# The last projection's column pair: other PSUM banks, and its first column's square sums and scalings behind the tail's splits

## The chip, the cores and the metric

The kernel runs on one core of a Trainium2 chip. The metric is the time of one execution on the device in microseconds (us). Before the change the median of three runs is 1376.21 us (1376.1 to 1376.72). A core has TensorE (PE, matrix products), VectorE (DVE), ScalarE (ACT), GpSimd (POOL) and SyncE (SP); the last two only issue transfers in the part of the program that matters here. Matrix products end in PSUM, 8 banks of 128 x 512 floats; VectorE and ScalarE read them from there.

## The reference

A trunk of two layers on 256 tokens of width 2048: one of gated linear attention, one of retention, each ahead of its own output projection and residual add, and one RMS norm at the end. The change touches only the last steps, in the second layer:

```python
    return (o * jax.nn.silu(gate)) @ w_out
...
            h = h + retention_mixer(rms_norm(h, ret_norm[j]), positions, ret_w_in[j],
                                    ret_gn_g[j], ret_gn_b[j], ret_w_out[j])
    return rms_norm(h, final_norm)
```

The final norm divides each token's row by the root of its mean square over all 2048 columns and multiplies by `final_norm`.

## The kernel before

**Precision.** A float32 product is done as three products of rounded parts. ScalarE rounds a weight block to its upper part (`hi`, L298), VectorE subtracts to get the lower part (`lo`, L299); this is "the split" of a weight block (128 x 1024, two k-tiles of 512 columns), written by `emit_split`. TensorE then multiplies x_hi by hi, x_hi by lo and x_lo by hi (L340 to L342 in `mm3`, L411 to L413 in `three`). So each step of TensorE needs `hi` for its first matmul and `lo` for its second. The `hi` and `lo` pools have four buffers each; splits are written up to three steps ahead (`LOOK`). Raw weight blocks come by transfers on SP's queue, each waiting for a buffer that a split has read; where two column blocks are combined, GpSimd's queue adds one block to another in a transfer (L310) or VectorE does (L293).

**The output projection.** Its 4096 rows are done in two halves of 2048; the last one (`out_last`, `out_tail`) makes four column blocks of 512 for two halves of tokens (t = 0, 1), and a step `j` covers 256 rows:
- column 0, steps 0 to 5; then column 3, steps 0 to 3 (`part`, 4 = `HEAD`); then column 0's last two steps. Column 3's part is added to the residual rows `rb_resid` at L1073, column 0's sums by `out_cols` (add L960, square sum L599, scaling by `final_norm` L964).
- columns 1 and 2 as a pair in `out_pair`, called with c = 1, g = 2. For the first half of its rows (steps 0 to 3) it makes seven products of sums and differences instead of eight (`product`, 12 matmuls each); the other steps 4 to 7 go directly (`direct`, 12 matmuls each). Four accumulators, B, A, C and V1, each take one PSUM bank: C and V1 gather column c, B and A gather column g, and A also serves for single products that are read at once. `join` adds a bank into `rb_resid` (L990) or subtracts (L992); `u3` is a copy of A by ScalarE (L1029).
- `whole(col, t)` finishes a block of a column: the square sum over it by ScalarE (L599, tile `sqj`, into `ssum`) and its scaling by `final_norm` on VectorE (L999).
- the tail: column 3's steps 4 to 7. Its four splits are written inside the pair, before direct step 7, in an extra loop: upper parts in `xhl`, lower ones in tiles `tail`. `out_tail` runs t = 0 in one bank (24 matmuls of 512) and t = 1 in two half-wide ones (48 of 256), and after each evacuates (L1142), squares (L1144), forms the norm factor from `ssum` by way of `pre` (L1121, L1122), scales the four columns (L1160, L1162) and sends them out.

**Banks.** The pool `acc` has four banks under the tags acc0 to acc3, one buffer each: a new tile under a tag waits until the old one has been read. `slots` says which tag comes next. When `out_pair` is reached, column 0's two halves (t = 0, 1) are in acc2 and acc3, and column 3's part, already added by L1073, in acc0 and acc1.

```python
        slots.rotate(1)
        B, A, C, V1 = acc(4, f"{name}e{c}_ps", which=list(slots))
...
    slots = deque((1, 2, 3, 0))
```

The first two lines stand ahead of the pair, the last one ahead of the tail. So B, A, C, V1 are acc1, acc2, acc3, acc0, and the tail uses acc1 for t = 0, acc2 and acc3 for t = 1.

**Order.** A scheduler puts the instructions of each engine in order by its own estimate of their times; `keep` pins an instruction to the order in which it is written. Joins, the tail's splits and the pair's matmuls are pinned; square sums and scalings are not.

Of the kernel before, what the change touches and what calls it, by code (L numbers as in the profile page):

```python
# [15 lines left out]
ALU = mybir.AluOpType  # L16
# [162 lines left out]
def kernel(  # L179
# [18 lines left out]
    nc = tc.nc  # L198
# [20 lines left out]
    keep = tc.keep_in_program_order  # L219
# [9 lines left out]
    slots = deque(range(4))  # L229
# [13 lines left out]
    def block(key):  # L243
        return w_all[places[key]].rearrange("p (k n) -> p k n", n=GW)
# [21 lines left out]
    def emit_raws(c):  # L266
        c = cur["load"] = max(c, cur.get("load", 0))
        while emitted["raw"] < len(loads):
            n = emitted["raw"]
            h = held.get(bufs[n])  # L270
            if n > c and (n > c + DMA_LOOK + len(_spare(loads[n])) or (h is not None and last_use[h] >= emitted["sub"])):
                break
            emit_raw()

    def split_tiles(i):
        if i < last0:
            hi = hi_p.tile([P, SUB, GW], F32R, tag="hi", name=f"hi{i}")
            lo = lo_p.tile([P, SUB, GW], F32R, tag="lo", name=f"lo{i}")
            return hi, lo
        j = i - last0  # L280
        hi = xhl[:, j * SUB : (j + 1) * SUB].rearrange("p k a t -> p k (a t)")
        return hi, t4_p.tile([P, SUB, GW], F32R, tag="t4", name=f"tail{j}")

    def emit_split(pieces=1, between=None):
        i = emitted["sub"]
        c, pre, post = subs[i]
        emit_raws(c)
        src = raws[c]
        for n in range(i + 1, min(i + 1 + EARLY, len(subs))):
            at, by = subs[n][:2]  # L290
            if by is not None and n not in added:
                added.add(n)
                nc.vector.tensor_tensor(raws[at], raws[at], raws[by], ALU.add)  # L293
        hi, lo = split_tiles(i)
        step = SUB // pieces
        for k in range(pieces):
            sl = slice(k * step, (k + 1) * step)
            a = nc.scalar.activation(hi[:, sl], src[:, sl], AF.Copy)  # L298
            b = nc.vector.tensor_tensor(lo[:, sl], src[:, sl], hi[:, sl].bitcast(F32), ALU.subtract)  # L299
            if i >= last0 - 4:  # L300
                keep(a)
                keep(b)
            if i == 0:
                first(a, b)
                if k == 0:
                    between()
        splits[i] = (hi, lo)
        emitted["sub"] += 1
        for n, key in post:
            nc.gpsimd.dma_start(raws[n], block(key), accum_op=ALU.add)  # L310
        emit_raws(c)
# [13 lines left out]
    def drain_side():  # L325
        while side:
            advance()

    def next_weights():
        i = state["sub"]  # L330
        while emitted["sub"] <= min(i + LOOK, len(subs) - 1):
            emit_split()
        state["sub"] += 1
        return splits.pop(i)
# [72 lines left out]
    def three(ps, xh, xl, hi, lo, q, stop):  # L407
        start, again = id(ps) not in begun, {"skip_group_check": id(ps) in closed}
        begun.add(id(ps))
        pin = keep if cur.get("pin") else lambda x: x  # L410
        pin(mm(ps, xh, hi[:, q, :], start=start, stop=False, **again))  # L411
        pin(mm(ps, xh, lo[:, q, :], start=False, stop=False, **again))  # L412
        pin(mm(ps, xl, hi[:, q, :], start=False, stop=stop, **again))  # L413
        if stop:
            closed.add(id(ps))
# [8 lines left out]
    def direct(lhs, ps, j, stop=False):  # L424
        hi, lo = next_weights()
        for t in range(2):
            cols = slice(t * P, (t + 1) * P)
            for q in range(SUB):
                kt = j * SUB + q
                three(ps[t], lhs[:, kt, 0, cols], lhs[:, kt, 1, cols], hi, lo, q, stop and q == SUB - 1)  # L430
# [47 lines left out]
    def get_resid(name):  # L478
        r = rs_p.tile([P, 2, D], F32, tag="rs", name=name)
        nc.gpsimd.dma_start(r, cur["resid_at"])  # L480
        cur["resid"] = r
# [56 lines left out]
    def first(*ins):  # L538
        for x in ins:
            tc.stamp_issue_order_token(x.ins, "first")  # L540
# [55 lines left out]

    def square_sum(t, c):
        junk = sg_p.tile([P, GW], F32, tag="sg", name="sqj")
        nc.scalar.activation(  # L599
            junk, cur["resid"][:, t, c * GW : (c + 1) * GW], AF.Square, accum_out=ssum[:, t, c : c + 1]  # L600
        )

# [363 lines left out]
    fns = {}  # L966
# [10 lines left out]
    def out_pair(c, first, name, final=False):  # L977
        lhs, s = ogt, cur["s"]
        B, A, C, V1 = acc(4, f"{name}e{c}_ps", which=list(slots))
        slots.rotate(-2)  # L980
        onward = not (first or final)
        P5 = lev_p.tile([P, GW], F32, tag="lev", name=f"{name}e{c}_p5")
        plain = lambda kt0, t: lambda k, a: lhs[:, kt0 + k, a, t * P : (t + 1) * P]
        summed = lambda i: lambda k, a: s[i][:, k, a, :]
        u3 = t4_p.tile([P, 2, GW], F32, tag="t4", name=f"{name}e{c}_u3")[:, 0, :]

        def join(col, t, src, op=ALU.add):
            dst = cur["resid"][:, t, col * GW : (col + 1) * GW]
            if op == ALU.add:
                keep(nc.vector.tensor_tensor(dst, src, dst, ALU.add))  # L990
            else:
                keep(nc.vector.tensor_tensor(dst, dst, src, ALU.subtract))  # L992

        def whole(col, t):
            if not first:
                square_sum(t, col)
            if final:
                dst = cur["resid"][:, t, col * GW : (col + 1) * GW]
                nc.vector.tensor_tensor(dst, dst, fns[col], ALU.mult)  # L999

        late = deque([out_transposes(c)] if onward else [])

        def turn():
            advance()
            if late:
                next(late[0], None)

        g = c + 1
        cur["pin"] = final
        product(A, plain(0, 0), stop=True)  # L1010
        advance()
        direct(lhs, (C, V1), 4)
        join(g, 0, A)
        advance()
        product(C, summed(0))
        advance()
        direct(lhs, (C, V1), 5)
        drain_side()
        product(P5, summed(1), stop=True)
        direct(lhs, (C, V1), 6)  # L1020
        for t in range(2):
            join(c, t, P5)
        product(A, summed(2), stop=True)
        product(B, plain(4, 0))
        join(c, 0, A, ALU.subtract)
        direct(lhs, (C, V1), 7, stop=True)
        product(A, summed(3), stop=True)
        with tc.high_priority():
            keep(nc.scalar.activation(u3, A, AF.Copy))  # L1029
        join(c, 0, C)  # L1030
        whole(c, 0)
        direct(lhs, (B, A), 4)
        join(c, 1, u3, ALU.subtract)
        join(c, 1, V1)
        whole(c, 1)
        direct(lhs, (B, A), 5)
        turn()
        product(A, plain(4, 1))
        turn()
        direct(lhs, (B, A), 6)  # L1040
        turn()
        while final and emitted["sub"] < len(subs):
            emit_split()
        direct(lhs, (B, A), 7, stop=True)
        join(g, 0, B)
        whole(g, 0)
        join(g, 1, A)
        whole(g, 1)
        if onward:
            for _ in late[0]:  # L1050
                pass
            tasks.append(out_transposes(g))
        begun.clear()
        closed.clear()
# [5 lines left out]
    def out_last(name):  # L1060
        ps = acc(2, f"{name}0_ps")
        steps_x(ps, ogt, range(CUT), lambda j: step())
        part = acc(2, f"{name}3_ps")
        steps_x(part, ogt, range(HEAD), lambda j: step(), end=HEAD)
        get_resid(f"{name}_resid")
        for c in range(3):
            norm_row(c)
        steps_x(ps, ogt, range(CUT, NSUB), lambda j: step())
        while tasks:
            step()  # L1070
        for t in range(2):
            dst = cur["resid"][:, t, 3 * GW : 4 * GW]
            nc.vector.tensor_tensor(dst, part[t], dst, ALU.add)  # L1073
        for t in range(2):
            out_cols(0, ps[t], t, False, True)
        norm_row(3)
        slots.rotate(1)
        out_pair(1, False, name, True)

    def out_half(first, final, name, cut=0, hook=None, joint=(False, False)):  # L1080
# [357 lines left out]
    slots = deque((2, 3, 0, 1))  # L1438
    out_half(True, False, "ga", joint=JOINT["ao", 0])
    slots = deque((2, 3, 0, 1))  # L1440
# [4 lines left out]
    slots = deque((2, 3, 0, 1))  # L1445
# [8 lines left out]
    slots = deque((0, 1, 2, 3))  # L1454
# [7 lines left out]
    slots = deque((2, 3, 0, 1))  # L1462
    tasks.append(make_sums(ogt, "rsum2", sums_in_v))
    out_last("rb")
    slots = deque((1, 2, 3, 0))
# [104 lines left out]
```

## Time and profile before

| | us |
|---|---|
| median of three runs | 1376.21 |
| the profiled execution | 1375.77 |
| its span, first to last instruction | 1374.0 |
| TensorE busy in the span | 1362.7 (99%) |
| VectorE busy | 1100.2 (80%) |
| ScalarE busy | 846.5 (62%) |
| the last pair on TensorE, first to last start | 1311.69 to 1353.19 |
| the tail on TensorE, first to last start | 1354.44 to 1365.60 |

Times of the trace count from the span's start. A row of the timeline names start, length, engine, line and operation, output and inputs, with the idle time of the engine just ahead of it in brackets and what ended it. Matmuls overlap: one of 512 columns takes 0.39 us, but the next starts 0.23 us after it, so their rate is read from the starts.

### The profile page before, as it was taken

To read this page: it belongs to the slowest core of one execution; us is meant where nothing else is said; L and a number is where in the kernel's file an instruction comes from. 1 tells how busy PE (TensorE), PEld (TensorE's weight loads), DVE (VectorE), ACT (ScalarE), POOL (GpSimd) and SP (SyncE) were. 2 spreads that over 40 slices of the span, in tenths; PEclk is the share of its full clock that TensorE was granted. 3 is DMA by queue.
4 is the path that set the end of the run, shared out by engine and by line. 5 is a ranking of instruction groups with operands and counts; after the bars stand their busy time and mean duration, and the time that the engine had idled before them with its cause. 6 is when DMAs were issued, how large, how long until landed. Compare 5 with 4: busy or idle time off the path is not lost.

```text
span 1374.0 us, 18376 instructions
## 1 busy us (share of the span) xinstructions
PE 1362.7 (99%) x6564; PEld 1143.6 (83%) x6564; DVE 1100.2 (80%) x1523; ACT 846.5 (62%) x1115; POOL 136.8 (10%) x194
## 2 busy tenths in 40 slices
PE   9999999999999999999999999999999999999997
PEld 7888888888888888888888888888888888888886
DVE  6686795987878886769888888886858897889786
ACT  6576656656567747656666566655546666666554
POOL 1003020110021021001011010100101101010010
PEclk9999999999999999999999999999999999999999
DMA  9755566789658667868897878896798797879772
GB/s 369 250 171 168 173 202 184 162 246 323 191 155 271 198 206 191 303 168 241 277 312 200 257 204 248 208 327 205 185 361 236 214 273 191 262 194 332 221 181 107
DMA packets 84507, 315.03 MB, mean 229 GB/s; under 512 B 9776, under 2 KB 10800, under 8 KB 83136
## 3 DMA queue, kind: packets, MB, share of 16 engines
q1 hardware_dynamic: 67200, 241.63, 50.6%
q0 software_dynamic: 15920, 64.89, 24.0%
q10 hardware_dynamic: 1296, 7.35, 1.5%
q8 instruction: 51, 0.84, 0.2%
q14 instruction: 40, 0.33, 0.1%
HBM read 303.35 MB, written 10.49 MB: 228 GB/s over the span
## 4 chain that ended last, share of the span: by engine, by line
PE 96%; DMA 1%; DVE 1%; issue 1%; ACT 0%; POOL 0%; SPq 0%; DVEq 0%; POOLq 0%; ACTq 0%
PE rqk_ps L383 8%; PE re_ps L411 8%; PE re_ps L412 8%; PE re_ps L413 8%; PE rqk_ps L384 4%; PE gqk_ps L383 4%; PE gg_ps L341 3%; PE gv_ps L342 3%; PE gv_ps L340 3%; PE gv_ps L341 3%; PE gg_ps L340 3%; PE gg_ps L342 3%; PE ge_ps L412 2%; PE ge_ps L411 2%; PE ge_ps L413 2%; PE gae_ps L413 2%
## 5 line engine op out<-in xcount | busy, mean ns | idle before, releaser
L299 DVE TENSOR_TENSOR lo<-raw,hi 128x1024 fp32r<-128x1024 f32 (+1 forms) x567 | 687.2, 1222 | 213.7 <-ACT hi L298 202.9
L298 ACT ACTIVATE hi<-raw 128x1024 fp32r<-128x1024 f32 (+1 forms) x567 | 596.5, 1057 | 391.8 <-PE rqk_ps L383 48.7
L383 PE MATMUL rqk_ps<-xhl,hi 128*128 128x512 f32 x480 | 162.8, 397 | 0.0
L412 PE MATMUL re_ps<-lo,xhl 128*128 128x512 f32 x352 | 137.4, 390 | 0.0
L413 PE MATMUL re_ps<-hi,xhl 128*128 128x512 f32 x352 | 137.2, 390 | 0.0
L310 POOL DMA_DIRECT2D raw<-in_w_all x90 | 78.0, 868 | 556.3 <-DVE lo L299 291.0
L411 PE MATMUL re_ps<-hi,xhl 128*128 128x512 f32 x352 | 132.5, 391 | 0.0
L384 PE MATMUL rqk_ps<-xhl,lo 128*128 128x256 f32 x480 | 122.4, 280 | 0.0
L383 PEld LDWEIGHTS rqk_ps<-xhl,hi 128*128 128x128 f32 x480 | 89.6, 188 | 17.8
L384 PEld LDWEIGHTS rqk_ps<-xhl,lo 128*128 128x128 f32 x480 | 87.6, 189 | 3.4
L413 PEld LDWEIGHTS re_ps<-hi,xhl 128*128 128x128 f32 x352 | 66.1, 188 | 13.6
L412 PEld LDWEIGHTS re_ps<-lo,xhl 128*128 128x128 f32 x352 | 66.1, 188 | 13.2
L411 PEld LDWEIGHTS re_ps<-hi,xhl 128*128 128x128 f32 x352 | 66.0, 188 | 13.3
L383 PE MATMUL gqk_ps<-xhl,hi 128*128 128x512 f32 x216 | 76.6, 399 | 0.0
L341 PE MATMUL gg_ps<-lo,xhl 128*128 128x512 f32 x192 | 75.4, 393 | 0.0
L341 PE MATMUL gv_ps<-lo,xhl 128*128 128x512 f32 x192 | 75.2, 392 | 0.0
L340 PE MATMUL gv_ps<-hi,xhl 128*128 128x512 f32 x192 | 75.1, 393 | 0.0
L342 PE MATMUL gv_ps<-hi,xhl 128*128 128x512 f32 x192 | 75.1, 391 | 0.0
L342 PE MATMUL gg_ps<-hi,xhl 128*128 128x512 f32 x192 | 75.0, 391 | 0.0
L340 PE MATMUL gg_ps<-hi,xhl 128*128 128x512 f32 x192 | 74.8, 391 | 0.0
L828 POOL TENSOR_TENSOR s<-s,m 128x64 f32<-128x64 f32 x56 | 36.2, 676 | 232.6 <-DVE m L819 223.3
L384 PE MATMUL gqk_ps<-xhl,lo 128*128 128x256 f32 x216 | 59.1, 280 | 0.0
(434 smaller groups left out, 2656.6 us busy)
## 6 DMA issues: line engine op xcount, KB each, us to landing
raw<-in_w_all SPq DMA_DIRECT2D x449, 512.0 KB, 4.8
raw<-in_w_all POOLq DMA_DIRECT2D x90, 512.0 KB, 6.8
resid<-in_x_n SPq DMA_DIRECT2D x2, 1024.0 KB, 10.4
gg<-in_gn_g POOLq DMA_DIRECT2D x8, 256.0 KB, 4.2
resid_x<-resid ACTq DMA_DIRECT2D x1, 2048.0 KB, 8.0
gb<-in_gn_b POOLq DMA_DIRECT2D x8, 256.0 KB, 6.3
gb_resid<-resid_x POOLq DMA_DIRECT2D x1, 2048.0 KB, 11.4
resid_g<-gb_resid ACTq DMA_DIRECT2D x1, 2048.0 KB, 9.1
```

What stands on the lines that cost most here:

```text
L298: a = nc.scalar.activation(hi[:, sl], src[:, sl], AF.Copy)
L299: b = nc.vector.tensor_tensor(lo[:, sl], src[:, sl], hi[:, sl].bitcast(F32), ALU.subtract)
L310: nc.gpsimd.dma_start(raws[n], block(key), accum_op=ALU.add)
L340: pin(mm(ps, xh, hi[:, q, :], start=kt == begin, stop=False))
L341: pin(mm(ps, xh, lo[:, q, :], start=False, stop=False))
L342: pin(mm(ps, xl, hi[:, q, :], start=False, stop=kt == end - 1))
L383: mm(ps[c], wh, rhs[:, kt, :, :], start=kt == 0, stop=False)
L384: mm(ps[c][:, 0, :], wl, rhs[:, kt, 0, :], start=False, stop=False)
L411: pin(mm(ps, xh, hi[:, q, :], start=start, stop=False, **again))
L412: pin(mm(ps, xh, lo[:, q, :], start=False, stop=False, **again))
L413: pin(mm(ps, xl, hi[:, q, :], start=False, stop=stop, **again))
L828: nc.gpsimd.tensor_tensor(dst, dst, side_of(m[:, li, :], z), ALU.add)
```

## The change

`rotate(1)` becomes `rotate(-1)`: B, A, C, V1 are now acc3, acc0, acc1, acc2. The tail's banks stay what they were, so it now follows C (t = 0) and V1 and B (t = 1) in its banks. And in the last pair, `whole` of column c is held back: its two square sums and two scalings are written after the tail's splits, ahead of direct step 7, and are pinned, as are column g's.

```diff
     def square_sum(t, c):
         junk = sg_p.tile([P, GW], F32, tag="sg", name="sqj")
-        nc.scalar.activation(
+        return nc.scalar.activation(
             junk, cur["resid"][:, t, c * GW : (c + 1) * GW], AF.Square, accum_out=ssum[:, t, c : c + 1]
         )
...
-        def whole(col, t):
+        held_back = []
+
+        def whole(col, t, now=False):
+            if final and col == c and not now:
+                held_back.append((col, t))
+                return
             if not first:
-                square_sum(t, col)
+                a = square_sum(t, col)
             if final:
+                keep(a)
                 dst = cur["resid"][:, t, col * GW : (col + 1) * GW]
-                nc.vector.tensor_tensor(dst, dst, fns[col], ALU.mult)
+                keep(nc.vector.tensor_tensor(dst, dst, fns[col], ALU.mult))
...
         while final and emitted["sub"] < len(subs):
             emit_split()
+        for col, t in held_back:
+            whole(col, t, True)
         direct(lhs, (B, A), 7, stop=True)
...
-        slots.rotate(1)
+        slots.rotate(-1)
         out_pair(1, False, name, True)
```

On all engines the instructions are the same as before. SP's, GpSimd's and TensorE's stand in the same order; on ScalarE and VectorE only the two square sums and the two scalings move. Lines from 994 on have other numbers in the changed kernel (L999 is L1005, L1142 is L1150). The numbers behind a name count tiles and differ between the kernels too.

VectorE before, from C's join in the pair (`rbe_ps_11571`) to the join of B (`rbe_ps_11569`); `fn_11516` is column c's part of `final_norm`:

```order
L990 TENSOR_TENSOR rb_resid<-rbe_ps_11571,rb_resid 128x512
L999 TENSOR_TENSOR rb_resid<-rb_resid,fn_11516 128x512
L299 TENSOR_TENSOR lo_11789<-raw_11331,hi_11788 128x1024
L992 TENSOR_TENSOR rb_resid<-rb_resid,rbe_u_11574 128x512
L990 TENSOR_TENSOR rb_resid<-rbe_ps_11572,rb_resid 128x512
L999 TENSOR_TENSOR rb_resid<-rb_resid,fn_11516 128x512
L299 TENSOR_TENSOR lo_11810<-raw_11640,hi_11809 128x1024
L299 TENSOR_TENSOR lo_11826<-raw_11682,hi_11825 128x1024
L299 TENSOR_TENSOR tail_11835<-raw_11702,xhl 128x1024
L299 TENSOR_TENSOR tail_11844<-raw_11714,xhl 128x1024
L299 TENSOR_TENSOR tail_11859<-raw_11726,xhl 128x1024
L299 TENSOR_TENSOR tail_11862<-raw_11738,xhl 128x1024
```

`lo_11810` belongs to direct step 6 of B and A, `lo_11826` to step 7; B's join follows the last row. VectorE at the same place now:

```order
L990 TENSOR_TENSOR rb_resid<-rbe_ps_11571,rb_resid 128x512
L299 TENSOR_TENSOR lo_11786<-raw_11331,hi_11785 128x1024
L992 TENSOR_TENSOR rb_resid<-rb_resid,rbe_u_11574 128x512
L990 TENSOR_TENSOR rb_resid<-rbe_ps_11572,rb_resid 128x512
L299 TENSOR_TENSOR lo_11804<-raw_11640,hi_11803 128x1024
L299 TENSOR_TENSOR lo_11820<-raw_11682,hi_11819 128x1024
L299 TENSOR_TENSOR tail_11829<-raw_11702,xhl 128x1024
L299 TENSOR_TENSOR tail_11838<-raw_11714,xhl 128x1024
L299 TENSOR_TENSOR tail_11853<-raw_11726,xhl 128x1024
L299 TENSOR_TENSOR tail_11856<-raw_11738,xhl 128x1024
L1005 TENSOR_TENSOR rb_resid<-rb_resid,fn_11516 128x512 x2
L990 TENSOR_TENSOR rb_resid<-rbe_ps_11569,rb_resid 128x512
```

Both scalings have gone from between the joins and splits to behind the tail's four splits, and stand directly ahead of B's join. ScalarE's square sums move in the same way, from ahead of the upper splits `hi_11788` and `hi_11809` to behind the four that go to `xhl`, where all four of the pair now follow one another.

TensorE where the tail begins, with the engines whose semaphores a matmul waits for, before:

```order
L412 MATMUL rbe_ps_11570<-lo_11826,ogt 128x512
L413 MATMUL rbe_ps_11570<-hi_11825,ogt 128x512
L340 MATMUL tail_ps_11889<-xhl,ogt 128x512 [waits DVE_49,Activation_49]
L341 MATMUL tail_ps_11889<-tail_11835,ogt 128x512
L342 MATMUL tail_ps_11889<-xhl,ogt 128x512
```

and now:

```order
L412 MATMUL rbe_ps_11570<-lo_11820,ogt 128x512
L413 MATMUL rbe_ps_11570<-hi_11819,ogt 128x512
L340 MATMUL tail_ps_11889<-xhl,ogt 128x512 [waits Activation_49]
L341 MATMUL tail_ps_11889<-tail_11829,ogt 128x512 [waits DVE_49]
L342 MATMUL tail_ps_11889<-xhl,ogt 128x512
```

The tail's first matmul waited for VectorE's read of the bank as well as for its upper split; now it waits for the split alone, and the second one for its lower split. At the pair's start the wait for a bank moves likewise, from A's first matmul to V1's first, 18 matmuls later.

## Prediction

> **What bounds the kernel now.** I read the page first (its chain), then TensorE's waits over the last 74 us, where the change lies, then TensorE's rows around each wait, then VectorE's and ScalarE's rows in front of them. The chain says that TensorE sets the time:
>
> ```profile
> span 1374.0 us, 18376 instructions
> ...
> PE 96%; DMA 1%; DVE 1%; issue 1%; ACT 0%; POOL 0%; SPq 0%; DVEq 0%; POOLq 0%; ACTq 0%
> ```
>
> So only what makes TensorE stand still, or what follows its last matmul, is worth anything. TensorE's waits from 1300 us to the end are three (us in total, times, longest):
>
> ```profile
> PE tail_ps L340 <- DVE rb_resid L990: 0.9, 1, 0.9
> PE rbe_ps L412 <- DVE lo L299: 0.5, 1, 0.5
> PE rbe_ps L411 <- DVE rb_resid L960: 0.4, 1, 0.4
> ```
>
> All three lie inside the last pair or at its two edges. TensorE's rows around them (start us, us, what, idle before and what ended it):
>
> ```profile
> 1310.92 0.39 PE L342 MATMUL rb_ps<-hi,ogt 128*128 128x512 f32 x1
> 1311.69 0.47 PE L411 MATMUL rbe_ps<-hi,ogt 128*128 128x512 f32 x1 [0.38 <-DVE rb_resid L960]
> ...
> 1312.24 0.39 PE L413 MATMUL rbe_ps<-hi,ogt 128*128 128x512 f32 x1
> ...
> 1347.16 0.39 PE L411 MATMUL rbe_ps<-hi,ogt 128*128 128x512 f32 x1
> 1348.07 0.50 PE L412 MATMUL rbe_ps<-lo,ogt 128*128 128x512 f32 x1 [0.53 <-DVE lo L299]
> 1348.41 0.40 PE L413 MATMUL rbe_ps<-hi,ogt 128*128 128x512 f32 x1
> 1348.64 0.39 PE L411 MATMUL rbe_ps<-hi,ogt 128*128 128x512 f32 x1
> ...
> 1353.19 0.39 PE L413 MATMUL rbe_ps<-hi,ogt 128*128 128x512 f32 x1
> 1354.44 0.47 PE L340 MATMUL tail_ps<-xhl,ogt 128*128 128x512 f32 x1 [0.86 <-DVE rb_resid L990]
> ...
> 1354.98 0.39 PE L342 MATMUL tail_ps<-xhl,ogt 128*128 128x512 f32 x1
> ```
>
> The idle in brackets is less than a pause costs, since the first matmul behind it also starts its successor late. I therefore measure by starts. Undisturbed, starts are 0.227 us apart: between 1312.24 and 1347.16 lie 154 steps (13 steps of 12 matmuls, less two), and 34.92 / 154 = 0.2268. A pause is then the third start behind it, less the last start ahead, less 3 x 0.227 = 0.68:
> - pause 1, at the pair's start: 1312.24 - 1310.92 - 0.68 = 0.64
> - pause 2, at the lower split of direct step 6: 1348.64 - 1347.16 - 0.68 = 0.80
> - pause 3, at the tail's first matmul: 1354.98 - 1353.19 - 0.68 = 1.11
>
> Together 2.55 us. Between them TensorE has no more to give, as the table by stage shows (stretch, us, TensorE busy, weight loads, VectorE, ScalarE, GpSimd, granted clock, DMA share):
>
> ```profile
> 1312.00:1347.00 35.00, 35.00 (x156) 28.98 (x155) 29.80 (x32) 21.49 (x28) 4.03 (x5) 1.00 0.75 201
> 1354.40:1365.80 11.40, 11.36 (x72) 10.32 (x72) 6.53 (x21) 5.39 (x14) 0.00 (x0) 1.00 0.15 55
> ```
>
> **The change, part by part.** VectorE's rows that the three pauses hang on, and those behind:
>
> ```profile
> 1310.87 1.28 DVE L960 TENSOR_TENSOR rb_resid<-rb_ps,rb_resid 128x512 f32<-128x512 f32 x2
> ...
> 1340.07 0.68 DVE L990 TENSOR_TENSOR rb_resid<-rbe_ps,rb_resid 128x512 f32<-128x512 f32 x1
> 1341.55 0.69 DVE L999 TENSOR_TENSOR rb_resid<-rb_resid,fn 128x512 f32<-128x512 f32 x1 [0.79 <-ACT sqj L599]
> 1342.50 1.23 DVE L299 TENSOR_TENSOR lo<-raw,hi 128x1024 fp32r<-128x1024 f32 x1 [0.26 <-ACT hi L298]
> 1343.64 0.68 DVE L992 TENSOR_TENSOR rb_resid<-rb_resid,rbe_u 128x512 f32<-128x512 f32 x1
> 1344.36 0.69 DVE L990 TENSOR_TENSOR rb_resid<-rbe_ps,rb_resid 128x512 f32<-128x512 f32 x1
> 1345.84 0.69 DVE L999 TENSOR_TENSOR rb_resid<-rb_resid,fn 128x512 f32<-128x512 f32 x1 [0.79 <-ACT sqj L599]
> 1346.79 2.36 DVE L299 TENSOR_TENSOR lo<-raw,hi 128x1024 fp32r<-128x1024 f32 x2 [0.26 <-ACT hi L298]
> 1349.07 4.63 DVE L299 TENSOR_TENSOR tail<-raw,xhl 128x1024 fp32r<-128x1024 f32 x4
> 1353.61 0.69 DVE L990 TENSOR_TENSOR rb_resid<-rbe_ps,rb_resid 128x512 f32<-128x512 f32 x1
> ...
> 1358.08 0.15 DVE L1122 TENSOR_SCALAR pre<-pre 128x1 f32<-128x1 f32 x1
> 1360.17 0.76 DVE L1142 TENSOR_TENSOR rb_resid<-tail_ps,rb_resid 128x256 f32<-128x256 f32 x2 [1.94 <-PE tail_ps L342]
> ```
>
> *Banks at the pair's start (pause 1).* A's first product used to need the bank that L960 empties at 1310.87 to 1311.55; now it takes one that column 3's part left long before. The L960 bank goes to V1, whose first matmul is the 19th of the pair: 1311.15 + 18 x 0.227 = 1315.23, 3.7 us after it is free. Pause 1 goes whole: 0.64.
>
> *Supply between 1312 and 1347.* This gain lasts only if splits keep up with a TensorE that is 0.64 us ahead. ScalarE's and the transfers' rows:
>
> ```profile
> 1332.95 2.01 ACT L298 ACTIVATE hi<-raw 128x1024 fp32r<-128x1024 f32 x2 [0.85 <-DMA raw<-in_w_all]
> ...
> 1339.20 0.60 ACT L1029 ACTIVATE rbe_u<-rbe_ps 128x512 f32<-128x512 f32 x1 [0.30 <-PE rbe_ps L413]
> 1340.79 0.63 ACT L599 ACTIVATE sqj<-rb_resid 128x512 f32<-128x512 f32 x1 [0.99 <-DVE rb_resid L990]
> ...
> 1345.71 1.99 ACT L298 ACTIVATE hi<-raw 128x1024 fp32r<-128x1024 f32 x2
> 1347.61 3.89 ACT L298 ACTIVATE xhl<-raw 128x1024 fp32r<-128x1024 f32 x4
> ...
> 1357.27 1.28 ACT L1118 ACT_TABLE_LOAD   x1
> ```
>
> ```profile
> 1327.25 12.83 DMA raw<-in_w_all
> ```
>
> ```profile
> DMA packets 2, 0.02 MB, mean 1 GB/s; under 512 B 0, under 2 KB 0, under 8 KB 0
> ```
>
> The first row is the one split here that a transfer held up; its data go to the second half of the sixth product, which begins with the pair's 115th matmul, so TensorE wants the lower split at 1312.24 + 113 x 0.2268 = 1337.9. The split pair ends by about 1335.3 (hi at 1334.0, 1.2 more for the lower). With TensorE 0.64 ahead, 2.0 us remain: no cost. The last accumulated transfer (next fence) lands at 1327.25 + 12.83 = 1340.08. The last fence is all DMA from 1344.5 to 1363: two small packets, so every weight block of the tail has landed by 1344.5. No DMA is moved, and the queues of SP and GpSimd keep their order.
>
> *Square sums and scalings of the first column moved (pause 2).* Before, VectorE loses in front of direct step 6's lower split two scalings (0.6 each by starts) and two waits of 0.79 for the square sums; ScalarE loses 0.73 for each sum ahead of an upper split. In the changed order, with TensorE 0.64 earlier (times in the clock of these rows):
> - TensorE: direct 4 at 1339.00 - 0.64 = 1338.36, direct 6 at 1346.52 with its lower split wanted at 1346.75, the tail at 1346.52 + 24 x 0.227 = 1351.97.
> - ScalarE: the copy u3 ends 1339.16; the next upper split waits for the data, 1340.1 to 1341.15; that of direct 6 for the buffer which direct 4 frees, 1341.3 to 1342.35; that of direct 7 for direct 5, 1344.0 to 1345.05; four tail splits (3.89) to 1348.95; the two held-back sums to 1350.4.
> - VectorE: lower split 1341.2 to 1342.3, joins L992 and L990 to 1343.6, direct 6's lower split 1343.6 to 1344.8: 1.9 us before TensorE wants it. Pause 2 goes whole: 0.80. Direct 7's follows 1345.1 to 1346.25, the four tail splits to 1350.9, the two scalings to 1352.1.
>
> *Banks at the tail (pause 3).* The tail's first half used to need the bank of B, whose join at 1353.61 stood behind four tail splits. It now takes C's bank, emptied by the join at 1340.07, and its upper splits are ready at 1346. Its second half needs V1's bank and B's; B's join, now from about 1352.1 to 1352.8, ends 4.6 us ahead of that (1351.97 + 24 x 0.227 = 1357.4). Pause 3 goes whole: 1.11.
>
> *What the moved work costs.* Two sums (1.46 on ScalarE) and two scalings (1.2 on VectorE) now stand ahead of B's join. Before, 4.62 us passed from that join (1353.61) to the last preparation (1358.08 + 0.15); the same from 1352.1 ends at 1356.7. The tail's first evacuation, 1360.17 before, is due at 1357.62. So of VectorE's 1.94 us of idle there 0.9 remain, and the cost is nothing. The table load ended 4.94 behind the join, now 1357.0, also in time. If that cover were gone, each us late would delay the first half's output, not TensorE. Behind TensorE's end every step keeps its place.
>
> What no row shows is how exactly a pause vanishes once its cause does: nothing returns at best (2.55), and at worst one of the three stays, the largest of which leaves 1.44. I take 2.55, since each margin (3.7, 1.9, 4.6 us) is over twice its pause.
>
> Does a pause also cost clock? Behind pause 2 starts are 0.34 and then 0.23 us apart, and the granted clock is 1.00 in both stretches above; so I add nothing for it. [...]
>
> **Sum.** 0.64 + 0.80 + 1.11 = 2.55. The profiled execution took 1375.77, so 1373.22; the median of the runs is 1376.21, which gives 1373.66, say 1373.7, or 0.19% less. Measurement can tell about 0.2% (2.75 us, below 1373.46) from no change; the forecast lies just inside.
>
> **Rivals.**
> - *The split stays late.* Should the data of 1340.08 land 1.9 us later, direct 6 waits again. Then only the bank part counts: 0.64 + 1.11 = 1.75, 1374.5. For it: that transfer took 12.83. Against it: it is issued behind a split that also moves earlier. 0.07.
> - *Pause 1 is given back to a transfer.* Weights come at DMA's pace, and ScalarE did wait 0.85 for one. It decides from 2.0 us late on; 1.91 remain, 1374.3. 0.05.
> - *Slower: the accumulating transfer is crowded out.* Loads asked for 0.64 us earlier share the engines with the transfer at 1327.25. Its data feed the seventh product's second half, the pair's 151st matmul on, whose lower split is wanted at 1346.0 - 0.64 = 1345.4; split takes 2.3, so there are 3.0 us to spare. From 3.0 + 2.55 = 5.5 us late on the kernel is slower than before, at 8.3 late by 0.2%: 1379.0. Against it: 12.83 would have to become 21. 0.03.
> [...]
> - *The order stays what it was,* and nothing moves: 1376.2. The rows of the changed order speak against it. 0.01.
>
> **How the numbers follow.** The forecast has 0.83. The runs scatter by 0.62 (1376.1 to 1376.72) and the profiled one lies 0.44 below their median, so a median of the changed kernel lies within some 0.5 of 1373.7; 1373.46 is only 0.2 away, and I put 0.31 of the 0.83 below it. Faster 0.31 + 0.01 = 0.32; same 0.52 + 0.07 + 0.05 + 0.01 = 0.65; slower 0.03. The range reaches down to 1372.9 (the forecast with its scatter) and up to 1374.8 (the largest pause stays: 1376.21 - 1.44).
>
> **What would show it.** TensorE's waits after 1300 us should be gone, all three; starts should stay 0.227 us apart from the pair's first matmul to the tail's 24th. The lower split of direct 6 should end two us before its matmul; the two scalings should stand behind four tail splits, and VectorE should idle about 0.9 us in front of the tail's first evacuation. A wait of TensorE on a lower split or a DMA, or a first evacuation that VectorE is late for, would prove a step wrong.

## The result and the profile after

The changed kernel takes 1373.85 us (median of 22 runs, 1373.05 to 1376.85); the kernel before, timed beside it, 1376.77 (22 runs, 1376.0 to 1381.1). The ratio is 0.9979, 95% interval 0.9973 to 0.9986, or 1.9 to 3.7 us less. The profiled execution took 1373.05 us, with a span of 1371.3.

The page of the changed kernel, its span, busy times and the chain that ended last by engine:

```profile
span 1371.3 us, 18373 instructions
PE 1362.1 (99%) x6564; PEld 1144.2 (83%) x6564; DVE 1099.5 (80%) x1523; ACT 845.8 (62%) x1115; POOL 136.8 (10%) x194
...
PE 99%; DVE 0%; ACT 0%; issue 0%; DVEq 0%; POOL 0%; POOLq 0%
```

TensorE is as busy as before within 0.6 us (1362.1 against 1362.7), while the span is 2.7 us shorter: most of what went is time in which it stood. The chain's 99% for TensorE, against 96% before, is no measure of the change: a second profile of this same program has 95%. The view of its waits over the whole run has one line left, at the warm-up, and none of the three that the prediction began with:

```profile
PE warm_ps L520 <- POOL lnone L522: 1.0, 1, 1.0
```

TensorE's rows (start, length, ...) from column 0's last matmul through the pair to the tail's last one:

```profile
1310.79 0.39 PE L342 MATMUL rb_ps<-hi,ogt 128*128 128x512 f32 x1
1311.02 0.39 PE L411 MATMUL rbe_ps<-hi,ogt 128*128 128x512 f32 x1
...
1351.59 0.39 PE L413 MATMUL rbe_ps<-hi,ogt 128*128 128x512 f32 x1
1351.82 0.39 PE L340 MATMUL tail_ps<-xhl,ogt 128*128 128x512 f32 x1
...
1362.89 0.28 PE L342 MATMUL tail_ps<-xhl,ogt 128*128 128x256 f32 x1
```

The pair starts 0.23 us behind column 0 and the tail 0.23 us behind the pair. The table by stage (stretch, us, TensorE busy, weight loads, VectorE, ScalarE, GpSimd, granted clock, DMA share) shows TensorE busy in every part at a clock of 1.00:

```profile
1311.50:1346.50 35.00, 35.00 (x156) 29.01 (x155) 31.25 (x32) 22.91 (x26) 4.03 (x5) 1.00 0.76 202
1346.50:1351.80 5.30, 5.30 (x25) 4.38 (x24) 5.30 (x6) 3.43 (x7) 0.00 (x0) 1.00 0.00 0
1351.80:1363.00 11.20, 11.20 (x73) 10.21 (x71) 7.17 (x23) 5.32 (x14) 0.00 (x0) 1.00 0.15 54
```

VectorE's rows from C's join in the pair to the norm's factor of the tail's first half (`fin`):

```profile
1339.29 0.68 DVE L990 TENSOR_TENSOR rb_resid<-rbe_ps,rb_resid 128x512 f32<-128x512 f32 x1
1340.81 1.23 DVE L299 TENSOR_TENSOR lo<-raw,hi 128x1024 fp32r<-128x1024 f32 x1 [0.83 <-ACT hi L298]
1341.95 0.68 DVE L992 TENSOR_TENSOR rb_resid<-rb_resid,rbe_u 128x512 f32<-128x512 f32 x1
1342.67 0.69 DVE L990 TENSOR_TENSOR rb_resid<-rbe_ps,rb_resid 128x512 f32<-128x512 f32 x1
1343.28 1.22 DVE L299 TENSOR_TENSOR lo<-raw,hi 128x1024 fp32r<-128x1024 f32 x1
...
1346.09 4.62 DVE L299 TENSOR_TENSOR tail<-raw,xhl 128x1024 fp32r<-128x1024 f32 x4
1350.63 1.28 DVE L1005 TENSOR_TENSOR rb_resid<-rb_resid,fn 128x512 f32<-128x512 f32 x2
1351.84 0.68 DVE L990 TENSOR_TENSOR rb_resid<-rbe_ps,rb_resid 128x512 f32<-128x512 f32 x1
...
1357.45 0.76 DVE L1150 TENSOR_TENSOR rb_resid<-tail_ps,rb_resid 128x256 f32<-128x256 f32 x2 [0.99 <-PE tail_ps L342]
1359.97 0.21 DVE L1120 TENSOR_SCALAR fin<-nf_nw 128x1 f32<-128x1 f32 x1
```

ScalarE's rows that the supply hangs on, and the table load of the norm:

```profile
1339.71 1.06 ACT L298 ACTIVATE hi<-raw 128x1024 fp32r<-128x1024 f32 x1 [0.70 <-DMA raw<-in_w_all]
...
1355.50 1.28 ACT L1126 ACT_TABLE_LOAD   x1
```

The two scalings stand behind the four tail splits and ahead of B's join, and VectorE no longer waits for a square sum ahead of a lower split.

### The profile page after: what moved, and what is told of

It reads as the page before. It is cut to its first block, busy times and chain, and to the rows that moved or that the text cites. A ratio compares the mean times of both kernels' runs of the same rounds, so it can differ in the third digit from the quotient of the medians.

```text
span 1371.3 us, 18373 instructions
## 1 busy us (share of the span) xinstructions
PE 1362.1 (99%) x6564; PEld 1144.2 (83%) x6564; DVE 1099.5 (80%) x1523; ACT 845.8 (62%) x1115; POOL 136.8 (10%) x194
## 4 chain that ended last, share of the span: by engine, by line
PE 99%; DVE 0%; ACT 0%; issue 0%; DVEq 0%; POOL 0%; POOLq 0%
PE rqk_ps L383 8%; PE re_ps L411 8%; PE re_ps L412 8%; PE re_ps L413 8%; PE rqk_ps L384 4%; PE gqk_ps L383 4%; PE gg_ps L341 3%; PE gv_ps L342 3%; PE gv_ps L340 3%; PE gv_ps L341 3%; PE gg_ps L340 3%; PE gg_ps L342 3%; PE ge_ps L413 2%; PE ge_ps L411 2%; PE ge_ps L412 2%; PE gae_ps L413 2%
## 5 line engine op out<-in xcount | busy, mean ns | idle before, releaser
L411 PEld LDWEIGHTS re_ps<-hi,xhl 128*128 128x128 f32 x352 | 66.0, 188 | 13.2
L342 PE MATMUL gv_ps<-hi,xhl 128*128 128x512 f32 x192 | 75.0, 391 | 0.0
L342 PE MATMUL gg_ps<-hi,xhl 128*128 128x512 f32 x192 | 74.9, 390 | 0.0
```

The source lines that it names most:

```text
L342: pin(mm(ps, xl, hi[:, q, :], start=False, stop=kt == end - 1))
```

## The experiments

**How they are read.** The whole time scatters by more than the terms in question: the profiled executions of before, 1375.77 and 1378.01, differ by 2.24 us. So each kernel is read by one stretch of its profile, from the start of column 0's last matmul (the last one with output rb_ps, L342, ahead of the pair) to the start of the tail's last matmul. TensorE's matmuls ahead of it are the same, in the same order, in all ten profiles. In us, each from the two rows of that kernel, as quoted for after above (1362.89 - 1310.79 = 52.10):

| kernel | from | to | length | less than before |
|---|---|---|---|---|
| before | 1310.92 | 1365.60 | 54.68 | |
| before_again | 1313.14 | 1367.86 | 54.72 | |
| start_bank_only | 1312.50 | 1366.55 | 54.05 | 0.63 |
| tail_bank_only | 1313.40 | 1367.00 | 53.60 | 1.08 |
| banks_only | 1312.37 | 1365.31 | 52.94 | 1.74 |
| hold_only | 1311.43 | 1365.14 | 53.71 | 0.97 |
| after | 1310.79 | 1362.89 | 52.10 | 2.58 |
| after_again | 1313.25 | 1365.35 | 52.10 | 2.58 |
| unpinned | 1312.04 | 1364.16 | 52.12 | 2.56 |
| four_more | 1312.19 | 1364.29 | 52.10 | 2.58 |

The two kernels that were profiled twice give the same length within 0.04, although "from" lies anywhere in 2.6 us. The theory is the prediction's: the gain is three pauses of TensorE with two causes, the banks (first and third) and the moved work (second). The rivals are that the moved work does it all or nothing, that it takes the pins of the order, that a bank's gain is given back elsewhere, or that the difference of times comes from somewhere else than this stretch.

### The banks alone

Edit to the kernel before:

```diff
-        slots.rotate(1)
+        slots.rotate(-1)
```

> The kernel before with rotate(-1) alone; square sums and scalings stay where they were. Theory (three pauses that add up: 0.64 us bank at the pair's start, 0.80 split of direct step 6, 1.11 bank at the tail): pauses 1 and 3 gone, pause 2 still there with about 0.8 us, so 1.75 us less than before (ratio 0.9987, profiled about 1374.0). Rival A (the banks are the whole gain, the split was late only because of the earlier pause): no pause left, 2.55 us less. Rival B (what pause 1 gives is given back at pause 2, because VectorE does not move along): pause 2 grows to 1.4 us, 1.1 us less.

Measured: 1375.28 us (11 runs, 1373.86 to 1377.79) beside 1376.6 for before (33 runs, 1375.41 to 1380.43), ratio 0.9992 (0.9984 to 1.0001), so the whole time cannot tell it from no change. The stretch is 1.74 shorter. Of TensorE's waits one is left in the stretch. Its rows there, and VectorE's row of C's join:

```profile
1347.96 0.39 PE L411 MATMUL rbe_ps<-hi,ogt 128*128 128x512 f32 x1
1348.87 0.50 PE L412 MATMUL rbe_ps<-lo,ogt 128*128 128x512 f32 x1 [0.52 <-DVE lo L299]
...
1349.44 0.40 PE L411 MATMUL rbe_ps<-hi,ogt 128*128 128x512 f32 x1
```

```profile
1340.87 0.68 DVE L990 TENSOR_TENSOR rb_resid<-rbe_ps,rb_resid 128x512 f32<-128x512 f32 x1
```

The first and third pause are gone, the second is there at its old length (1349.44 - 1347.96 - 0.68 = 0.80). It did not grow to 1.4, because VectorE's work in front of it moved along: C's join comes 1340.87 - 1312.37 = 28.50 behind column 0's last matmul, against 1340.07 - 1310.92 = 29.15 before. The difference from here to after, 52.94 - 52.10 = 0.84, is what the moved work is worth on top of the banks.

### The moved work alone

Edit to the changed kernel:

```diff
-        slots.rotate(-1)
+        slots.rotate(1)
```

> The changed kernel with the old rotate(1): square sums and scalings held back, banks as before. Theory: pause 1 stays (0.64), pause 2 gone (0.80 gained); the tail still waits for B's bank, whose join now comes behind the four tail splits and the two scalings, at about 1352.6, with TensorE there at 1352.6: pause 3 shrinks only to about 0.9, so about 1.0 us less than before (ratio 0.9993, profiled about 1374.8). Rival A (banks are the whole gain): 0. Rival B (the scalings ahead of B's join cost the tail what pause 2 gave): pause 3 grows to 1.9, 0 gained.

Measured: 1376.06 us (11 runs, 1375.29 to 1377.74), ratio 0.9994 (0.9986 to 1.0003). The stretch is 0.97 shorter, more than the second pause alone. The two waits of TensorE in the stretch:

```profile
PE tail_ps L340 <- DVE rb_resid L990: 0.7, 1, 0.7
PE rbe_ps L411 <- DVE rb_resid L960: 0.4, 1, 0.4
```

TensorE at the tail, and VectorE's rows there:

```profile
1352.90 0.39 PE L413 MATMUL rbe_ps<-hi,ogt 128*128 128x512 f32 x1
1353.98 0.47 PE L340 MATMUL tail_ps<-xhl,ogt 128*128 128x512 f32 x1 [0.69 <-DVE rb_resid L990]
...
1354.52 0.39 PE L342 MATMUL tail_ps<-xhl,ogt 128*128 128x512 f32 x1
```

```profile
1351.94 1.29 DVE L1005 TENSOR_TENSOR rb_resid<-rb_resid,fn 128x512 f32<-128x512 f32 x2
1353.15 0.68 DVE L990 TENSOR_TENSOR rb_resid<-rbe_ps,rb_resid 128x512 f32<-128x512 f32 x1
```

The third pause is here 1354.52 - 1352.90 - 0.68 = 0.94 instead of 1.11, although the two scalings now stand directly ahead of B's join. They stood ahead of it before, too, only further up, and the waits for square sums that went with them there are gone. That 0.17 is why the two halves add up to 1.74 + 0.97 = 2.71 and the whole is 2.58: once the banks remove the third pause, shortening it is worth nothing.

### The changed kernel once more

No edit.

> The changed kernel as it is, beside the others on one chip. Theory: no wait of TensorE after 1300 us, 2.55 us less than before (ratio 0.9981). If more than the three pauses is gained, the ratio stays at 0.9979 or below and the profile has to show another place that is shorter than before by 0.3 us or more.

Measured: 1374.27 us (11 runs, 1373.2 to 1376.14), ratio 0.9982 (0.9973 to 0.9991). The profiled execution took 1375.52, 2.47 more than the first profile of the same program, and the stretch is the same to the hundredth. TensorE's rows at the two waits that the first profile did not have:

```profile
9.88 1.19 PE L371 MATMUL gqk_ps<-xhl,hi 128*128 128x512 f32 x4 [1.53 <-ACT hi L298]
...
1191.39 0.50 PE L412 MATMUL re_ps<-lo,sums 128*128 128x512 f32 x1 [0.53 <-DVE lo L299]
```

The extra time lies ahead of the pair, where column 0's last matmul comes 1313.25 - 1310.79 = 2.46 later. Counted from start to start, 1.30 of it is there behind the run's first weights (the first matmul into zps starts at 13.12 instead of 11.82; the wait shows 1.53, but the first products had started earlier here). The split in the middle costs 0.81: from the start ahead of its wait to the third start behind it 1190.48 to 1192.19, against 1189.01 to 1189.91 in the first profile. Some 0.35 is spread over smaller steps. The pair and its edges are free of waits in both, so nothing beyond the three pauses is gained.

### The same order, not pinned

Edit to the changed kernel: the sums and scalings are still written behind the tail's splits, but the scheduler may move them.

```diff
-                keep(a)
...
-                keep(nc.vector.tensor_tensor(dst, dst, fns[col], ALU.mult))
+                nc.vector.tensor_tensor(dst, dst, fns[col], ALU.mult)
```

> The changed kernel without the two pins on the square sums and scalings: they are still written behind the tail's splits, and the scheduler puts them back among the splits (a sum behind the upper split of the product's second half and one behind that of direct step 6, a scaling ahead of V1's join and one behind direct step 6's lower split). Theory: what counts is that the upper split goes ahead of the sum; the scalings have 1.9 us of room, so no pause and the same time as the changed kernel (ratio 0.998). Rival (the pins are what matters): pause 2 is back with 0.8 us, ratio 0.9987.

Measured: 1374.32 us (11 runs, 1373.08 to 1375.42), ratio 0.9982 (0.9973 to 0.9991), stretch 52.12: the time of the changed kernel. But the order is not. ScalarE's rows:

```profile
1341.09 1.06 ACT L298 ACTIVATE hi<-raw 128x1024 fp32r<-128x1024 f32 x1 [0.81 <-DMA raw<-in_w_all]
1342.06 0.61 ACT L599 ACTIVATE sqj<-rb_resid 128x512 f32<-128x512 f32 x1
...
1342.67 1.04 ACT L298 ACTIVATE hi<-raw 128x1024 fp32r<-128x1024 f32 x1
1345.25 0.64 ACT L599 ACTIVATE sqj<-rb_resid 128x512 f32<-128x512 f32 x1 [1.54 <-DVE rb_resid L990]
```

And VectorE's:

```profile
1344.53 0.68 DVE L990 TENSOR_TENSOR rb_resid<-rbe_ps,rb_resid 128x512 f32<-128x512 f32 x1
1345.13 1.22 DVE L299 TENSOR_TENSOR lo<-raw,hi 128x1024 fp32r<-128x1024 f32 x1
1346.27 0.69 DVE L1004 TENSOR_TENSOR rb_resid<-rb_resid,fn 128x512 f32<-128x512 f32 x1
```

The scheduler put both sums and scalings back among the splits of the pair. What differs from before is that each upper split now stands ahead of the sum beside it (1341.09 ahead of 1342.06, 1342.67 ahead of 1345.25), and direct step 6's lower split ahead of the second scaling. So VectorE reaches that lower split at 1345.13 straight behind the join, and it ends at 1346.35. TensorE starts on it at 1347.88, so 1.5 us are to spare. Neither the pins nor a place behind all of the tail's splits is needed for the gain: it was enough here that the splits which TensorE wants next go ahead of the sums and scalings. Which of the two pairs of sum and scaling matters more was not tried.

### One bank at a time

Edit to the kernel before, for the pair's start alone: the other rotation, and the tail's slots shifted so that it again follows B in its first bank, as before.

```diff
-        slots.rotate(1)
+        slots.rotate(-1)
...
-    slots = deque((1, 2, 3, 0))
+    slots = deque((3, 0, 1, 2))
```

> The kernel before with rotate(-1) at the pair, and the tail's slots turned so that it still follows B in its first bank (tail slots 3, 0, 1, 2); no instruction moved. Times from start to start on TensorE, from the last matmul of column 0 to the tail's last: 54.68 us before. Theory: pause 1 goes (0.64), pause 2 (0.80) and pause 3 (1.11) stay, so about 54.04. Rival B (the gain is given back at pause 2 or 3, since VectorE's work in front of them is as long as before): 54.68.

Measured: one execution, 1376.69 us beside 1376.73; stretch 0.63 shorter. Its two waits in the stretch:

```profile
PE tail_ps L340 <- DVE rb_resid L990: 0.9, 1, 0.9
...
PE rbe_ps L412 <- DVE lo L299: 0.5, 1, 0.5
```

For the tail alone, only the second of the two edits, with which the tail follows C (t = 0) and V1 and B (t = 1), as in the changed kernel:

> The kernel before with the tail's slots 3, 0, 1, 2 alone: the tail's first half follows C in its bank instead of B; the pair's banks and the order stay. Theory: pause 1 (0.64) and pause 2 (0.80) stay, pause 3 goes (1.11): 53.57 us from column 0's last matmul to the tail's last, against 54.68. Rival (behind the bank the tail's first splits are late, too): a wait of the tail on VectorE's lower split, less than 1.11 gained.

Measured: one execution, 1377.17 us; stretch 1.08 shorter. Its two waits in the stretch:

```profile
PE rbe_ps L412 <- DVE lo L299: 0.5, 1, 0.5
...
PE rbe_ps L411 <- DVE rb_resid L960: 0.4, 1, 0.4
```

Each edit takes away the wait for its own bank and no other, and the two together (0.63 + 1.08 = 1.71) make banks_only's 1.74. As whole times these two executions say nothing: one is 0.04 us below the run of before beside it, the other 0.44 above.

### The kernel before once more

No edit.

> The kernel before, looked at again. Theory: the scatter of the runs comes from the program's first us (the first weights), so from column 0's last matmul to the tail's last it is again 54.68 us within 0.05, with the same three pauses, wherever the span ends. Rival (the scatter is in the pair): the three pauses differ by some tenths of a us.

Measured: one execution, 1378.01 us, stretch 54.72, with the three pauses as they were. Its "from" is 2.2 us later than in the first profile. The first weights account for 0.67 of that (the first matmul into zps starts at 12.61 instead of 11.93). Most of the rest came in two short waits in the middle that the first profile did not have:

```profile
993.37 0.50 PE L411 MATMUL rae_ps<-hi,ogt 128*128 128x512 f32 x1 [0.23 <-ACT hi L298]
994.28 0.50 PE L411 MATMUL rae_ps<-hi,rsum 128*128 128x512 f32 x1 [0.41 <-DVE ra_resid L992]
```

They show 0.64 us of idle and cost 1.20: from the start ahead of the first one to the third start behind the second, 992.75 to 995.08, against 992.03 to 993.16 in the first profile. The 0.3 us that is left comes nearly all between 1110 and 1125, with no wait shown. So the expected place of the scatter, the first weights, holds for less than a third of it.

### More work ahead of the tail's first evacuation

Edit to the changed kernel: behind each held-back scaling of the last pair, two more operations that leave the values as they are (max(x, x)).

```diff
             whole(col, t, True)
+            if final:
+                dst = cur["resid"][:, t, col * GW : (col + 1) * GW]
+                for _ in range(2):
+                    keep(nc.vector.scalar_tensor_tensor(dst, dst, 1.0, dst, ALU.mult, ALU.max))
```

> The changed kernel with four more operations on VectorE (x times 1 and the greater of it and x, on 128 x 512, which leave the values as they are) directly behind the two held-back scalings, ahead of B's join; about 0.65 us each, so 2.6 us. The scheduler puts some of the small operations of the tail in another order. Theory: TensorE is untouched (52.1 us from column 0's last matmul to the tail's last); the 0.99 us of VectorE's idle ahead of the tail's first evacuation is used up, that evacuation is about 1.6 us late, and the program's end, which had 1.13 us more to spare, is some 0.5 us later. Rival (the end hangs on VectorE already): 2.6 us later.

Measured: one execution, 1375.62 us, span 1373.9. TensorE's stretch is unchanged, 52.10. But the time from the tail's last start to the end of the span is 1373.9 - 1364.29 = 9.61, against 1371.3 - 1362.89 = 8.41 in after: 1.2 us, where about 0.5 was expected, and 2.6 if the end had hung on VectorE already. VectorE's rows:

```profile
1352.76 1.42 DVE L1055 SCALAR_TENSOR_TENSOR rb_resid<-rb_resid 128x512 f32<-128x512 f32 x2
...
1354.81 1.42 DVE L1055 SCALAR_TENSOR_TENSOR rb_resid<-rb_resid 128x512 f32<-128x512 f32 x2
...
1358.95 0.75 DVE L1154 TENSOR_TENSOR rb_resid<-tail_ps,rb_resid 128x256 f32<-128x256 f32 x2
1360.01 0.69 DVE L1005 TENSOR_TENSOR rb_resid<-rb_resid,fn 128x512 f32<-128x512 f32 x1
...
1363.89 0.42 DVE L1154 TENSOR_TENSOR rb_resid<-tail_ps,rb_resid 128x256 f32<-128x256 f32 x1 [1.01 <-PE tail_ps L342]
1364.23 0.20 DVE L1124 TENSOR_SCALAR fin<-nf_nw 128x1 f32<-128x1 f32 x1
...
1364.69 0.74 DVE L1172 TENSOR_SCALAR rb_resid<-rb_resid,fin 128x256 f32<-128x256 f32 x2
...
1365.75 0.42 DVE L1154 TENSOR_TENSOR rb_resid<-tail_ps,rb_resid 128x256 f32<-128x256 f32 x1
```

The four operations took the idle in front of the first evacuation, as expected, but the evacuation is not 1.6 us late: it starts 1358.95 - 1353.22 = 5.73 behind the tail's start, against 5.63 in after, with no idle ahead. The scheduler put it ahead of a 512-column scaling (1360.01) that stands before it in after, and the late work piled up behind it. The norm's factor of the first half comes 1364.23 - 1353.22 = 11.0 behind the tail's start instead of 8.15. Its last step now stands behind the second half's first evacuation, ahead of which VectorE sat idle for 1.01 us until TensorE's products were there. The factor's scalings (1364.69) then stand ahead of the last evacuation, which starts only at 1365.75, though TensorE ended at 1364.57. So in this run, with the 0.99 us in front of the first evacuation used up, VectorE's work behind the pair set the end. Part of the price is the order that the scheduler found, the 1.01 us of idle in it; what the excess alone would have cost was not tried.

## Why the prediction was right

**The sum.** 2.55 us was forecast from three pauses, and the stretch is 2.58 shorter in two profiles of the changed kernel. Each term was measured by itself: 0.64 for the pair's start is 0.63 in start_bank_only; 0.80 for direct step 6's lower split is 0.84, from banks_only to after; 1.11 for the tail's bank is 1.08 in tail_bank_only. A pause measured by starts, as the third start behind it, is worth that much; the idle in brackets (0.38, 0.53, 0.86: 1.77 in all) would have given 0.8 us too little.

**The margins.** None was used up, and each came out close. Against the first tail matmul at 1351.97 forecast stands 1351.82; B's join came at 1351.84, forecast 1352.1; VectorE's idle before the first evacuation is 0.99, forecast 0.9; the table load ended at 1356.78, forecast 1357.0. Direct step 6's lower split ended at 1344.5 and its matmul started at 1346.60, so 2.1 us were to spare where 1.9 was forecast.

**The rivals.** The accumulating transfer came no later: it took 13.2 us instead of 12.83, but was issued at 1326.47 instead of 1327.25. ScalarE still waited 0.70 for it, until 1339.71, 0.4 us earlier than it landed before (1340.08). Its lower split ended at about 1342.0 and its matmul started at 1345.24, 3.2 us to spare where 3.0 was forecast. So the slower rival did not come near its point of decision. Pause 1 was not given back: no wait of TensorE for a split is left in the pair. No run shows a gain of the clock, for which the chances have 0.01 beside the 0.31 of "faster": starts are 0.23 us apart at a granted clock of 1.00 on both sides of the change, and the mean granted clock of every profile, with the pauses or without them, is 0.998 or 0.999.

**What was mis-sized: the scatter.** The forecast of 1373.7 stands beside a median of 1373.85 and 1374.27 in the repeat. But the prediction took the runs' scatter as 0.62 from three executions. Over 22 it is 3.8 us for the changed kernel and 5.1 for the kernel before. That the forecast came within 0.2 us of the median is in part luck. Its base, 1376.21, was the median of three runs; the median of before is 1376.77 over 22, and from there the same 2.55 us would have led to 1374.2. The medians differ by 2.92 us in the first comparison and by 2.33 in the second, with the stretch's 2.58 between them. The scatter is also large enough to decide on which side of 0.2% a median falls. The first comparison gave 0.9979, just beyond that bound, with an interval that reaches to both sides of it; the second gave 0.9982, just inside. The two intervals overlap and both hold the 0.9981 that 2.58 us would make. Of the 2.72 us between the two first profiled executions, 2.58 came from the stretch and the rest (1310.92 - 1310.79 = 0.13, and 0.01 at the end) from places that the change does not touch.

**Not in the prediction.** It said nothing of whether the pins matter. They do not (unpinned): the gain of the second part was there as soon as the splits went ahead of the sums and scalings beside them.

## What to carry to other kernels

Where one engine bounds the kernel, look at the rows around each of its few waits and measure every pause from start to start, a few instructions past it. Here the three lengths (0.64, 0.80 and 1.11) made 2.55 us of the 2.58 gained; the two halves of the change did not add up (1.74 + 0.97 = 2.71), since the moved work also took 0.17 us off the pause at the tail in hold_only, which the banks remove whole. A bank that was asked for right behind the engine that empties it cost a pause at both places here, 0.63 and 1.08 us: give the next user a bank that has been free for longer, and look at both ends of the part whose banks change. When a gain is smaller than the scatter of whole runs, compare a stretch between two instructions that every version has; here the stretch repeated within 0.04 us, and 1.7 us could not be told from nothing in the whole time.

## What the runs showed that had not been expected

The scatter of the whole time arises far from the change. In all ten profiles TensorE does the same matmuls in the same order up to column 0's end, and yet the last of them starts anywhere between 1310.79 and 1313.40. One part is the run's first weights: TensorE's wait for an upper split there is nothing in one profile of the changed kernel and 1.53 us in the other, where ScalarE itself waited 1.50 us for the raw weights of that split. Another part are single waits of 0.2 to 0.7 us in the middle of the run. Some of their places are shared: hold_only and four_more both wait 0.2 us at 328, before_again and four_more for the same matmul, at 994.28 and 993.55. Measured from start to start, these waits cost more than the idle that they show (0.81 for 0.53, 1.20 for 0.64), as the three pauses did. What makes the transfers and these waits differ from run to run was not tried and stays open.
